# Gate2's modulation moved into quarters 1 and 2 of an MLP, and the last quarter's weight sums made by adding transfers

## The chip, the cores and the metric

The kernel runs on one core of a Trainium2 chip. The metric is the time of one execution on the device, in microseconds (us). Its engines are named here as in the profile: PE (TensorE, matrix products), DVE (VectorE), ACT (ScalarE), POOL (GpSimd), and SP (SyncE), whose queue issues the transfers. Sixteen DMA engines carry them out.

## The reference, cut to what matters

One layer of a decoder on 512 positions with 1024 features, in f32: a mixer (a recurrent branch and an attention branch, merged by gates), then an MLP with 4096 hidden features. The six vectors of the modulation come from one small product with a large weight matrix; `gate2` is the last of them and is used only in the last line.

```python
mod = (c_act @ w_ada[l] + b_ada[l])[:, None, :]
shift1, scale1, gate1, shift2, scale2, gate2 = jnp.split(mod, N_MOD, axis=-1)
...
x = x + gate1 * (merged @ w_out[l])

h2 = rms_norm(x) * (1.0 + scale2) + shift2
ff = jnp.square(jax.nn.relu(h2 @ w_ff1[l])) @ w_ff2[l]
x = x + gate2 * ff
```

## The kernel before, in words

Every f32 operand of a product is split into a high part (a cast to fp32r, on ACT) and a low part (the rest, on DVE); three matmuls, high x high, low x high and high x low, make one product (`mm3`, lines 127 to 131). A weight block of 128 x 1024 is loaded by SP into one of three slots (tag "w" of `wpool`), cast on ACT (`wh`, L122) and its rest taken on DVE (`wl`, L123), each with two buffers (`load_w`, lines 114 to 125).

The modulation is not computed on PE. `ada_chunk(j, k)` (lines 184 to 189) loads 128 x 1024 weights for 128 columns of vector j into a slot of the same tag "w" and multiplies and reduces them on DVE (L188) into one column of `mod`. j = 5 is gate2, of eight blocks; the column of block n is read at the very end, as `mcol(5, n)`.

The MLP goes in four quarters of 1024 hidden features (lines 1025 to 1040). In a quarter, `hidden` (858 to 868) computes eight hidden blocks f1_q_0 to f1_q_7 of 128 features by 512 positions; ACT applies relu and the square. Three blocks of the next quarter are computed ahead among the products, by `beside`, so that five remain in the hidden stage proper. Then `out_product` (870 to 1008) multiplies the quarter's hidden features by its share of `w_ff2`. This is a 2 x 2 block product with seven block products instead of eight (a Winograd scheme): p1 to p7 and sums of blocks. The four blocks of the hidden features are A[r][k] (256 positions by 512 features), the four of the weights b(k, c), each held in two tiles of 128 x 4 x 256 (512 KB each). The weights' sums are

- t1 = b(0,0) + b(0,1), for p5
- t2 = t1 + b(1,1), for p6
- t3 = b(0,1) + b(1,1), for p7
- t4 = t2 + b(1,0), for p4, which in the last quarter is `last_product`, called pl.

`sums` (945 to 948) makes them on DVE in place, two instructions (L948) each; b(0,0), b(1,0) and b(1,1) are used unsummed for p1, p2 and p3. The b tiles have eight slots (tag "b"), and a new quarter's tile takes a slot when the last reader of its old tile is done. `split_b` (893 to 907) splits each tile as above (L904 on ACT, L905 on DVE); the first tile of a product has two buffers of its own (p_0h, p_0l), the second shares those of `load_w` (p_1h, p_1l).

A product writes two PSUM banks X, Y or Z, and `add_c` (911 to 918) adds them on DVE to the f32 sums C[r][c][t] in SBUF. p5 goes to Z and p3 adds onto Z after C[1][1] has taken p5's result; X is used so by p1, p6, p7 and p4, Y by p2 (`second`). In quarter 3, p2 stands second, and at the end `finish` (1012 to 1023) transposes C on PE, multiplies by gate2 and adds to `x1` (L1020); `last_product` does the same with pl from PSUM (L941); both store to `out`.

The order on each engine is made by a scheduler, which takes the program's order and a priority: the casts, splits and sums stand inside `tc.high_priority(HP)` and are placed far ahead of their program order. Each engine then works its list strictly in order and waits at semaphores.

Of the kernel before, what the change touches and what calls it, by code (L numbers as in the profile page):

```python
# [16 lines left out]
F32 = mybir.dt.float32  # L17
# [4 lines left out]
ALU = mybir.AluOpType  # L22
AX = mybir.AxisListType

P = 128
S = 512
D = 1024
KC = D // P
# [25 lines left out]
def build(tc, out, x, xT_in, c, pos, vecs, reps, ada, w_xr, w_xr7, w_qk, w_v, w_gr, w_gm, w_lru,  # L54
          w_pr, w_pa, w_out, w_ff1, w_ff2):
    nc = tc.nc
    from contextlib import ExitStack

    with ExitStack() as es:
# [714 lines left out]
        acc = t_("acc", tag="a")  # L774
# [70 lines left out]
        ff = es.enter_context(tc.tile_pool(name="ff", bufs=1))  # L845
# [12 lines left out]
        def hidden(qd, ahead):  # L858

            raw = [ff.tile([P, 4, S], F32, name=f"r2_{qd}_{c}", tag="raw", bufs=2) for c in range(2)]  # L860
            for n in range(KC):
                rl = raw[n // 4][:, n % 4, :]
                if n < len(ahead):
                    nc.scalar.activation(rl, ahead[n], AF.Square)
                else:
                    hidden_relu(qd, n, rl)
                    nc.scalar.activation(rl, rl, AF.Square)
            return raw

        def out_product(qd, raw, beside):  # L870
            A = [[raw[k][:, :, r * H2:(r + 1) * H2] for k in range(2)] for r in range(2)]
            B = {}

            def get_b(k, c):
                if (k, c) not in B:
                    B[k, c] = []
                    for hf in range(2):
                        b = ff.tile([P, 4, 2 * P], F32, name=f"b{qd}_{k}{c}{hf}", tag="b", bufs=8)
                        k0 = (4 * k + 2 * hf) * P
                        nc.sync.dma_start(b, w_ff2[qd, 4 * c:4 * c + 4, :, k0:k0 + 2 * P].rearrange("n p f -> p n f"))  # L880
                        B[k, c].append(b)
                return B[k, c]

            def split_a(src, name, parts=1):
                ah = ff.tile([P, 4, H2], F32R, name=f"{name}h{qd}", tag="ah", bufs=3)
# [34 lines left out]
            def product(name, a, bs, ps, first):  # L920

                fs = [split_b(b, f"{name}_{qd}_{i}", i) for i, b in enumerate(bs)]
                for hf in range(2):
                    for t in range(2):
                        for kk in range(2):
                            k = 2 * hf + kk
                            ts = slice(t * P, (t + 1) * P)
                            mm3(ps[t], a[0][:, k, ts], a[1][:, k, ts], fs[hf][0][:, kk], fs[hf][1][:, kk],
                                first and k == 0, k == 3, not first)

            def last_product(a, bs):

                fs = [split_b(b, f"pl_{i}", i) for i, b in enumerate(bs)]
                for n in range(4):
                    ps = bank(f"pl{n}")[:, :H2]
                    fc = slice(n * P, (n + 1) * P)
                    for k in range(4):
                        wh, wl = (w[:, k % 2, fc] for w in fs[k // 2])
                        mm3(ps, wh, wl, a[0][:, k], a[1][:, k], k == 0, k == 3)
                    cols = slice(H2, S)  # L940
                    nc.vector.scalar_tensor_tensor(x1[n][:, cols], ps, mcol(5, n), x1[n][:, cols],  # L941
                                                   op0=ALU.mult, op1=ALU.add)
                    nc.sync.dma_start(out[n][:, cols], x1[n][:, cols])

            def sums(dsts, srcs):
                with tc.high_priority(HP):
                    for d, s_ in zip(dsts, srcs):
                        nc.vector.tensor_tensor(d, d, s_, op=ALU.add)  # L948
# [16 lines left out]

            if qd == 3:
                second()
            b12 = get_b(0, 1)
            sums(b11, b12)
            Z = [bank(f"Z{qd}_{t}") for t in range(2)]  # L970
            product("p5", s1, b11, Z, True)
            beside()
            with tc.high_priority(HP):
                nc.vector.tensor_tensor(sx, sx, A[0][0], op=ALU.subtract)
                s2 = split_a(sx, "s2")
            add_c(1, 1, Z, 1)
            b22 = get_b(1, 1)
            sums(b11, b22)
            product("p6", s2, b11, X, False)
            beside()  # L980
            with tc.high_priority(HP):
                nc.vector.tensor_tensor(sx, sx, A[0][1], op=ALU.add)
                s4 = split_a(sx, "s4")
            add_c(0, 1, X, -1)
            product("p3", s4, b22, Z, False)
            nc.vector.tensor_tensor(A[0][0], A[0][0], A[1][0], op=ALU.subtract)
            s3 = split_a(A[0][0], "s3")
            add_c(0, 1, Z, 1)
            sums(b12, b22)
            product("p7", s3, b12, X, False)  # L990
            add_c(1, 1, X, -1)
            if qd < 3:
                second()
            a22 = split_a(A[1][1], "a22")
            sums(b11, get_b(1, 0))
            if qd < 3:
                product("p4", a22, b11, X, False)
                add_c(1, 0, X, 1)
                return

# [4 lines left out]
                finish(n, 2, 4, False)  # L1005
            for n in range(4, KC):
                finish(n, 0, 4)
            last_product(a22, b11)

        n_fin = [0]  # L1010

# [13 lines left out]
        ahead = []  # L1025
        for qd in range(4):
            raw = hidden(qd, ahead)
            if qd == 0:
                for n in range(KC):
                    ada_chunk(5, n)  # L1030
            ahead = []

            def beside():

                if qd < 3:
                    ahead.append(t_(f"ahead{qd + 1}_{len(ahead)}"))
                    hidden_relu(qd + 1, len(ahead) - 1, ahead[-1])

            beside()
            out_product(qd, raw, beside)  # L1040
# [66 lines left out]
```

## Time and profile before

| | us |
|---|---|
| three timed runs | 893.14, 896.8, 897.4 (median 896.8) |
| the profiled execution, its own time | 894.77 |
| its span, first to last instruction | 893.0 |
| PE busy (share of the span) | 867.7 (97%) |
| DVE busy | 657.4 (74%) |
| ACT busy | 448.3 (50%) |
| POOL busy | 2.2 (0%) |

PE's granted clock is at its upper level nearly throughout (mean 0.998). The MLP begins near 555 us. Quarter 0's first product p1 starts at 595.8, quarter 3's at 843.2; quarters 1 and 2 are alike and 81.6 us apart.

How to read the rows below: a row of the timeline gives the start, the duration, the engine, the line, the operation with its tiles (output <- inputs, buffer numbers left out, so that p_0h stands for the first tile's high part of whatever product), and in brackets for how long the engine had been idle and what released it. Matmuls overlap, so that durations of single ones are longer than the spacing of their starts. A row with x2 holds two instructions in a row.

### The profile page before, as it was taken

The page shows a single profiled execution, that of the slowest core. Times are in us where ns is not written, and L with a number is a line of the kernel's source. Part 1 is how long each engine was busy: PE and PEld are TensorE (multiplying, and loading weights), DVE is VectorE, ACT ScalarE, POOL GpSimd, SP SyncE. Part 2 cuts the span into 40 slices and gives each one's busy share as a digit, 9 for nine tenths or more (in the row PEclk, how much of TensorE's full clock was granted, in tenths as well). Part 3 has the DMA queues.
Part 4 walks back from the last instruction along what each step waited for, and adds up shares of the span by engine and source line. Part 5 has one row for each costly group of instructions (what it writes and reads, how often), then busy time and mean ns, then how long its engine had stood idle before and what let it go on. Part 6 is the DMA issues. An engine that isn't in the chain of part 4 may idle for free.

```text
span 893.0 us, 11189 instructions
## 1 busy us (share of the span) xinstructions
PE 867.7 (97%) x4012; PEld 707.0 (79%) x4012; DVE 657.4 (74%) x1227; ACT 448.3 (50%) x748; POOL 2.2 (0%) x40
## 2 busy tenths in 40 slices
PE   6999999999999999999999999989999999999988
PEld 3888888687878878877778888878888888888867
DVE  6972983499969855895868566879646883876597
ACT  6663544895536533534543343746545544553541
POOL 0000000000000000000000000000000000000000
PEclk9999999999999999999999999999999999999999
DMA  8932236321255474448745332772421342233002
GB/s 318 353 142 97 92 116 144 120 70 48 95 127 158 137 213 146 142 136 206 246 155 183 135 119 78 273 237 95 163 99 48 118 142 95 72 117 118 1 1 94
DMA packets 54874, 121.56 MB, mean 136 GB/s; under 512 B 5666, under 2 KB 23202, under 8 KB 54820
## 3 DMA queue, kind: packets, MB, share of 16 engines
q1 hardware_dynamic: 54820, 120.87, 41.9%
q8 instruction: 31, 0.51, 0.2%
q14 instruction: 23, 0.19, 0.1%
HBM read 106.17 MB, written 2.10 MB: 121 GB/s over the span
## 4 chain that ended last, share of the span: by engine, by line
PE 74%; DVE 16%; DMA 5%; ACT 2%; issue 2%; SPq 0%; DVEq 0%; ACTq 0%
PE f L129 5%; PE f L130 5%; PE f L131 5%; DMA ada<-in_ada 3%; DVE wl L123 3%; PE X L131 3%; PE X L130 3%; PE X L129 3%; PE qk L131 2%; PE qk L129 2%; PE qk L130 2%; PE xr L129 2%; PE xr L131 2%; PE xr L130 2%; PE wo L130 2%
## 5 line engine op out<-in xcount | busy, mean ns | idle before, releaser
L122 ACT CAST wh<-w 128x1024 fp32r<-128x1024 f32 (+1 forms) x113 | 117.9, 1043 | 214.6 <-issue 56.2
L123 DVE TENSOR_TENSOR wl<-w,wh 128x1024 fp32r<-128x1024 f32 (+1 forms) x113 | 137.0, 1213 | 87.7 <-ACT wh L122 86.6
L129 PE MATMUL f<-h2h,wh 128*128 128x512 f32 x240 | 93.0, 390 | 2.3 <-ACT wh L122 2.3
L131 PE MATMUL f<-h2h,wl 128*128 128x512 f32 x240 | 93.5, 390 | 0.4 <-DVE wl L123 0.4
L130 PE MATMUL f<-h2l,wh 128*128 128x512 f32 x240 | 93.2, 389 | 0.0
L129 PEld LDWEIGHTS f<-h2h,wh 128*128 128x128 f32 x240 | 45.1, 188 | 12.0 <-ACT wh L122 2.7
L131 PEld LDWEIGHTS f<-h2h,wl 128*128 128x128 f32 x240 | 45.1, 188 | 10.0 <-DVE wl L123 0.8
L188 DVE CUSTOM_DVE_ANT_0 ada<-ada,cb,bada 128x1024 f32<-128x1024 f32 x32 | 41.0, 1281 | 16.1 <-DMA ada<-in_ada 16.1
L130 PEld LDWEIGHTS f<-h2l,wh 128*128 128x128 f32 x240 | 45.1, 188 | 9.3
L131 PE MATMUL gm<-hh,wl 128*128 128x512 f32 x128 | 51.3, 401 | 0.0
L129 PE MATMUL gm<-hh,wh 128*128 128x512 f32 x128 | 51.1, 399 | 0.0
L130 PE MATMUL gm<-hl,wh 128*128 128x512 f32 x128 | 50.9, 398 | 0.0
L129 PE MATMUL qk<-wh,hh 128*128 128x512 f32 x128 | 50.8, 398 | 0.0
L131 PE MATMUL qk<-wh,hl 128*128 128x512 f32 x128 | 50.6, 395 | 0.0
L130 PE MATMUL qk<-wl,hh 128*128 128x512 f32 x128 | 50.2, 393 | 0.0
L588 ACT ACTIVATE e<-e,nm 128x128 f32<-128x128 f32 (+3 forms) x64 | 35.8, 561 | 28.7 <-DVE nm L586 28.4
L905 DVE TENSOR_TENSOR p_1l<-b,p_1h 128x1024 fp32r<-128x1024 f32 x27 | 33.0, 1223 | 21.8 <-ACT p_1h L904 21.8
L904 ACT CAST p_0h<-b 128x1024 fp32r<-128x1024 f32 x27 | 28.5, 1054 | 27.2 <-PE X L131 14.0
L904 ACT CAST p_1h<-b 128x1024 fp32r<-128x1024 f32 x27 | 28.3, 1050 | 27.3 <-PE f L130 24.5
L905 DVE TENSOR_TENSOR p_0l<-b,p_0h 128x1024 fp32r<-128x1024 f32 x27 | 33.0, 1222 | 11.7 <-ACT p_0h L904 11.6
L948 DVE TENSOR_TENSOR b<-b,b 128x1024 f32<-128x1024 f32 x32 | 38.7, 1220 | 0.1
L586 DVE CUSTOM_DVE_ANT_0 e<-sc,mask 128x128 f32<-128x128 f32 (+3 forms) x64 | 30.3, 486 | 10.4 <-PE sc L581 10.4
(438 smaller groups left out, 2169.8 us busy)
## 6 DMA issues: line engine op xcount, KB each, us to landing
ada<-in_ada SPq DMA_DIRECT2D x32, 512.0 KB, 4.2
w<-in_w_ff SPq DMA_DIRECT2D x32, 512.0 KB, 3.2
b<-in_w_ff SPq DMA_DIRECT2D x32, 512.0 KB, 3.5
ada<-in_ada SPq DMA_DIRECT2D x32, 256.0 KB, 5.8
w<-in_w_qk SPq DMA_DIRECT2D x16, 512.0 KB, 3.3
w<-in_w_gm SPq DMA_DIRECT2D x16, 512.0 KB, 3.6
w<-in_w_gr SPq DMA_DIRECT2D x8, 512.0 KB, 3.2
w<-in_w_v SPq DMA_DIRECT2D x8, 512.0 KB, 3.2
```

The source lines that it names most:

```text
L122: i_w = nc.scalar.copy(wh[:, :n], w[:, :n])
L123: nc.vector.tensor_tensor(wl[:, :n], w[:, :n], f32(wh)[:, :n], op=ALU.subtract)
L129: nc.tensor.matmul(ps, lh, rh, start=first, stop=False, skip_group_check=more)
L130: nc.tensor.matmul(ps, lh, rl, start=False, stop=False, skip_group_check=more)
L131: nc.tensor.matmul(ps, ll, rh, start=False, stop=last, skip_group_check=more)
L188: nc.vector.tensor_tensor_reduce(w, w, cb, 1.0, bada[:, col:col + 1], op0=ALU.mult, op1=ALU.add, accum_out=mod[:, col:col + 1])
L586: nc.vector.tensor_tensor_reduce(e[:, :n], ps[m][:, :n], mask[:, S - n:], 1.0, 1e30, op0=ALU.add, op1=ALU.min, accum_out=nm)
L588: nc.scalar.activation(e[:, :n], e[:, :n], AF.Exp, bias=nm, scale=-1.0, accum_out=sums[:, m:m + 1])
L904: nc.scalar.copy(v4(wh), v)
L905: nc.vector.tensor_tensor(v4(wl), v, f32(v4(wh)), op=ALU.subtract)
L948: nc.vector.tensor_tensor(d, d, s_, op=ALU.add)
```

## The change

Two parts. The first takes gate2's eight `ada_chunk` calls from behind quarter 0's hidden stage and puts four each into `hidden` of quarters 1 and 2, one behind each of the hidden blocks 4 to 7. The second, in quarter 3 alone (`by_dma`), makes the sums t1, t2, t3 and t4 not on DVE: a fresh tile is loaded by SP with the first block, and further blocks are added into it by transfers that POOL issues with `accum_op=ALU.add`. t2 is loaded anew from b(0,0), and gets b(0,1) and b(1,1) one after the other; t4 adds b(1,0) into t2's tiles once p6 has split them. That makes twelve plain loads by SP instead of eight in this quarter, and ten adding transfers.

```diff
@@ -865,21 +865,48 @@
                 else:
                     hidden_relu(qd, n, rl)
                     nc.scalar.activation(rl, rl, AF.Square)
+                if qd in (1, 2) and n >= 4:
+                    ada_chunk(5, 4 * (qd - 1) + n - 4)
             return raw
 
         def out_product(qd, raw, beside):
             A = [[raw[k][:, :, r * H2:(r + 1) * H2] for k in range(2)] for r in range(2)]
             B = {}
 
+            def src_b(k, c, hf):
+                k0 = (4 * k + 2 * hf) * P
+                return w_ff2[qd, 4 * c:4 * c + 4, :, k0:k0 + 2 * P].rearrange("n p f -> p n f")
+
+            def load_b(name, *parts):
+
+                res = []
+                for hf in range(2):
+                    b = ff.tile([P, 4, 2 * P], F32, name=f"b{qd}_{name}{hf}", tag="b", bufs=8)
+                    nc.sync.dma_start(b, src_b(*parts[0], hf))
+                    for p_ in parts[1:]:
+                        nc.gpsimd.dma_start(b, src_b(*p_, hf), accum_op=ALU.add)
+                    res.append(b)
+                return res
+
             def get_b(k, c):
                 if (k, c) not in B:
-                    B[k, c] = []
-                    for hf in range(2):
-                        b = ff.tile([P, 4, 2 * P], F32, name=f"b{qd}_{k}{c}{hf}", tag="b", bufs=8)
-                        k0 = (4 * k + 2 * hf) * P
-                        nc.sync.dma_start(b, w_ff2[qd, 4 * c:4 * c + 4, :, k0:k0 + 2 * P].rearrange("n p f -> p n f"))
-                        B[k, c].append(b)
+                    B[k, c] = load_b(f"{k}{c}", (k, c))
                 return B[k, c]
+
+
+
+            by_dma = qd == 3
+
+            def b_sum(name, acc, k, c, *parts):
+
+                if not by_dma:
+                    sums(acc, get_b(k, c))
+                    return acc
+                if acc is None:
+                    return load_b(name, *parts, (k, c))
+                for hf, b in enumerate(acc):
+                    nc.gpsimd.dma_start(b, src_b(k, c, hf), accum_op=ALU.add)
+                return acc
 
             def split_a(src, name, parts=1):
                 ah = ff.tile([P, 4, H2], F32R, name=f"{name}h{qd}", tag="ah", bufs=3)
@@ -965,36 +992,34 @@
 
             if qd == 3:
                 second()
-            b12 = get_b(0, 1)
-            sums(b11, b12)
+            t1 = b_sum("t1", None if by_dma else b11, 0, 1, (0, 0))
             Z = [bank(f"Z{qd}_{t}") for t in range(2)]
-            product("p5", s1, b11, Z, True)
+            product("p5", s1, t1, Z, True)
             beside()
             with tc.high_priority(HP):
                 nc.vector.tensor_tensor(sx, sx, A[0][0], op=ALU.subtract)
                 s2 = split_a(sx, "s2")
             add_c(1, 1, Z, 1)
-            b22 = get_b(1, 1)
-            sums(b11, b22)
-            product("p6", s2, b11, X, False)
+            t2 = b_sum("t2", None if by_dma else t1, 1, 1, (0, 0), (0, 1))
+            product("p6", s2, t2, X, False)
             beside()
             with tc.high_priority(HP):
                 nc.vector.tensor_tensor(sx, sx, A[0][1], op=ALU.add)
                 s4 = split_a(sx, "s4")
             add_c(0, 1, X, -1)
-            product("p3", s4, b22, Z, False)
+            product("p3", s4, get_b(1, 1), Z, False)
             nc.vector.tensor_tensor(A[0][0], A[0][0], A[1][0], op=ALU.subtract)
             s3 = split_a(A[0][0], "s3")
             add_c(0, 1, Z, 1)
-            sums(b12, b22)
-            product("p7", s3, b12, X, False)
+            t3 = b_sum("t3", None if by_dma else get_b(0, 1), 1, 1, (0, 1))
+            product("p7", s3, t3, X, False)
             add_c(1, 1, X, -1)
             if qd < 3:
                 second()
             a22 = split_a(A[1][1], "a22")
-            sums(b11, get_b(1, 0))
+            t4 = b_sum("t4", t2, 1, 0)
             if qd < 3:
-                product("p4", a22, b11, X, False)
+                product("p4", a22, t4, X, False)
                 add_c(1, 0, X, 1)
                 return
 
@@ -1005,7 +1030,7 @@
                 finish(n, 2, 4, False)
             for n in range(4, KC):
                 finish(n, 0, 4)
-            last_product(a22, b11)
+            last_product(a22, t4)
 
         n_fin = [0]
 
@@ -1025,9 +1050,6 @@
         ahead = []
         for qd in range(4):
             raw = hidden(qd, ahead)
-            if qd == 0:
-                for n in range(KC):
-                    ada_chunk(5, n)
             ahead = []
 
             def beside():
```

SP's list in quarter 0 (w88 to w93 are f1 blocks, w89 that of f1_1_0; ada40 to ada47 are gate2's eight; b0 are weights of this quarter's products). Before:

```order
L118 DMA w88_5705<-in_w_ff1 128x1024
L187 DMA ada40_5738<-in_ada 128x1024
L880 DMA b0_101_6093<-in_w_ff2 128x4x256
L187 DMA ada41_5741<-in_ada 128x1024
...
L187 DMA ada47_5759<-in_ada 128x1024
L118 DMA w89_5763<-in_w_ff1 128x1024
L118 DMA w90_5891<-in_w_ff1 128x1024
```

Now, with the place in quarter 1 where three of the blocks went:

```order
L118 DMA w88_5705<-in_w_ff1 128x1024
L118 DMA w89_5739<-in_w_ff1 128x1024
L885 DMA b0_101_6069<-in_w_ff2 128x4x256
L118 DMA w90_5867<-in_w_ff1 128x1024
...
L885 DMA b1_101_6658<-in_w_ff2 128x4x256
L187 DMA ada41_6252<-in_ada 128x1024
L118 DMA w95_6255<-in_w_ff1 128x1024
L187 DMA ada42_6288<-in_ada 128x1024
L118 DMA w96_6291<-in_w_ff1 128x1024
L187 DMA ada43_6324<-in_ada 128x1024
L118 DMA w97_6328<-in_w_ff1 128x1024
```

w89 has moved ahead of all gate2 blocks; ada40 now stands behind the first block of quarter 1 (b1_000), and ada41 to ada43 alternate with f1 blocks. Quarter 2 has the same pattern with ada44 to ada47.

DVE's list in quarter 3, from the splits of p3 on (b3_000 and b3_001 hold t2, then t4; b3_010 and b3_011 hold t3). Before:

```order
L905 TENSOR_TENSOR p3_3_0l_7687<-b3_110_7641,p3_3_0h_7686 128x1024
L918 TENSOR_TENSOR C001_5525<-C001_5525,X3_1_7494 128x512
L905 TENSOR_TENSOR p3_3_1l_7691<-b3_111_7643,p3_3_1h_7690 128x1024
L948 TENSOR_TENSOR b3_000_7495<-b3_000_7495,b3_100_7556 128x1024
L948 TENSOR_TENSOR b3_001_7497<-b3_001_7497,b3_101_7558 128x1024
L905 TENSOR_TENSOR p7_3_0l_7728<-b3_010_7594,p7_3_0h_7727 128x1024
L918 TENSOR_TENSOR C000_5524<-C000_5524,Y3_0_7554 128x512
L905 TENSOR_TENSOR p7_3_1l_7732<-b3_011_7596,p7_3_1h_7731 128x1024
L918 TENSOR_TENSOR C001_5525<-C001_5525,Y3_1_7555 128x512
L918 TENSOR_TENSOR C110_5530<-C110_5530,Z3_0_7600 128x512
```

Now:

```order
L945 TENSOR_TENSOR C000_5524<-C000_5524,Y3_0_7554 128x512
L932 TENSOR_TENSOR p3_3_0l_7693<-b3_110_7688,p3_3_0h_7692 128x1024
L945 TENSOR_TENSOR C001_5525<-C001_5525,Y3_1_7555 128x512
L945 TENSOR_TENSOR C110_5530<-C110_5530,Z3_0_7600 128x512
L932 TENSOR_TENSOR p3_3_1l_7697<-b3_111_7690,p3_3_1h_7696 128x1024
L945 TENSOR_TENSOR C111_5531<-C111_5531,Z3_1_7601 128x512
L1011 TENSOR_TENSOR r2_3_0_7323<-r2_3_0_7323 128x4x256
L932 TENSOR_TENSOR p7_3_0l_7738<-b3_t30_7731,p7_3_0h_7737 128x1024
```

The sums are gone, and the additions of Y and Z into C have moved ahead of p7's splits. On PE the four transposes of C[0][0] have moved from behind p6 to behind p7, the product next to the last.

POOL's list, which before ended with the last of the memsets that write the rotary frequencies, long before the MLP; now it goes on with the ten adds, first tile and second tile of t1, t2 (twice), t3 and t4:

```order
L362 MEMSET fr_640 128x4 x32
L887 DMA b3_t10_7594<-in_w_ff2 128x4x256
L887 DMA b3_t11_7597<-in_w_ff2 128x4x256
L887 DMA b3_t20_7641<-in_w_ff2 128x4x256
L887 DMA b3_t21_7645<-in_w_ff2 128x4x256
...
L887 DMA b3_t30_7731<-in_w_ff2 128x4x256
L887 DMA b3_t31_7734<-in_w_ff2 128x4x256
L908 DMA b3_t20_7641<-in_w_ff2 128x4x256
L908 DMA b3_t21_7645<-in_w_ff2 128x4x256
```

The second add of each t2 tile waits for the first; t3's tiles take the slots that p1's and p2's second tiles leave.

## Rows read from the trace of the kernel before

**Rows 1.** Waits of PE, 555 us to the end: us in total, times, longest.

```profile
PE cT L1017 <- DVE C L918: 2.6, 2, 1.3
PE f L129 <- ACT wh L122: 2.3, 1, 2.3
PE f L131 <- DVE wl L123: 0.4, 1, 0.4
PE Z L129 <- DVE C L918: 0.3, 1, 0.3
```

**Rows 2.** Stretches: us, busy time of each engine, clock, DMA share, GB/s.

```profile
655.00:682.00 27.00, 27.00 (x120) 22.37 (x120) 8.20 (x9) 11.96 (x17) 0.00 (x0) 1.00 0.29 98
...
843.00:866.00 23.00, 22.27 (x98) 17.92 (x96) 21.68 (x22) 13.31 (x15) 0.00 (x0) 1.00 0.00 0
866.00:869.00 3.00, 0.92 (x5) 0.48 (x5) 3.00 (x5) 0.36 (x1) 0.00 (x0) 1.00 0.00 0
```

**Rows 3.** Timeline, quarter 0: start us, us, engine line op, idle before and releaser.

```profile
595.73 6.77 SPq L118 DMA_DIRECT2D w<-in_w_ff  x4
...
600.94 0.50 PE L129 MATMUL f<-h2h,wh 128*128 128x512 f32 x1 [2.29 <-ACT wh L122]
```

**Rows 4.** Timeline, DVE in quarter 3.

```profile
862.35 2.35 DVE L948 TENSOR_TENSOR b<-b,b 128x1024 f32<-128x1024 f32 x2
...
865.76 0.68 DVE L918 TENSOR_TENSOR C<-C,Y 128x512 f32<-128x512 f32 x1
...
867.53 0.68 DVE L918 TENSOR_TENSOR C<-C,Y 128x512 f32<-128x512 f32 x1
```

**Rows 5.** The page's groups, the reduction of a modulation block: busy us, mean ns.

```profile
L188 DVE CUSTOM_DVE_ANT_0 ada<-ada,cb,bada 128x1024 f32<-128x1024 f32 x32 | 41.0, 1281 | 16.1 <-DMA ada<-in_ada 16.1
```

**Rows 6.** Timeline, hidden stage of quarter 1: casts and split of f1 blocks.

```profile
658.21 1.05 ACT L122 CAST wh<-w 128x1024 fp32r<-128x1024 f32 x1 [3.62 <-PE f L130]
...
659.29 1.23 DVE L123 TENSOR_TENSOR wl<-w,wh 128x1024 fp32r<-128x1024 f32 x1 [3.94 <-ACT wh L122]
...
663.65 1.05 ACT L122 CAST wh<-w 128x1024 fp32r<-128x1024 f32 x1 [2.58 <-PE f L130]
```

**Rows 7.** The page's DMA issues: KB each, median us from issue to landing.

```profile
ada<-in_ada SPq DMA_DIRECT2D x32, 512.0 KB, 4.2
...
b<-in_w_ff SPq DMA_DIRECT2D x32, 512.0 KB, 3.5
...
w<-in_w_xr SPq DMA_DIRECT2D x8, 448.0 KB, 6.3
...
out_dram<-x SPq DMA_DIRECT2D x8, 128.0 KB, 1.7
```

**Rows 8.** Timeline, DVE in the tail.

```profile
879.06 2.65 DVE L918 TENSOR_TENSOR C<-C,X 128x512 f32<-128x512 f32 x4
881.63 0.87 DVE L1020 SCALAR_TENSOR_TENSOR x<-cT,mod,x 128x256 f32<-128x256 f32 x2
...
885.39 2.93 DVE L1020 SCALAR_TENSOR_TENSOR x<-cT,mod,x 128x512 f32<-128x512 f32 x4
...
889.35 0.48 DVE L941 SCALAR_TENSOR_TENSOR x<-pl,mod,x 128x256 f32<-128x256 f32 x1 [0.64 <-PE pl L131]
```

**Rows 9.** Timeline, b blocks of quarter 3: loads, splits and casts.

```profile
799.49 0.37 SPq L880 DMA_DIRECT2D b<-in_w_ff  x1
...
807.95 0.37 SPq L880 DMA_DIRECT2D b<-in_w_ff  x1
...
844.25 1.23 DVE L905 TENSOR_TENSOR p_1l<-b,p_1h 128x1024 fp32r<-128x1024 f32 x1 [1.70 <-ACT p_1h L904]
...
857.21 1.22 DVE L905 TENSOR_TENSOR p_1l<-b,p_1h 128x1024 fp32r<-128x1024 f32 x1
...
865.31 1.04 ACT L904 CAST p_1h<-b 128x1024 fp32r<-128x1024 f32 x1 [1.21 <-PE X L131]
...
874.87 1.04 ACT L904 CAST pl_1h<-b 128x1024 fp32r<-128x1024 f32 x1
```

## The prediction

> **What bounds the kernel now.** I read the waits of TensorE (PE) over the MLP first, then the busy times in stretches around them, and last the timeline at the two places where PE waits; elsewhere in the MLP PE's work is dense and only its amount counts, which the change leaves as it is. From 555 us to the end PE waits for four causes [rows 1]: 2.3 + 0.4 us for a weight block's split in quarter 0, and 2.6 + 0.3 us for additions into C by VectorE (DVE) in quarter 3. A hidden stage (655 to 682) has no wait, PE is busy 27.00 of 27 us and DVE 8.20; at 866 to 869 it is the other way round, DVE 3.00 of 3.00 and PE 0.92, and before it DVE has worked 21.68 of 23 us [rows 2]. The granted clock is 1.00 (the 2.4 GHz level) in all of them.
>
> Quarter 0: SyncE (SP) issues the eight gate2 blocks first, each when one of the three shared slots is free, and only at 595.73 the block of f1_1_0, which PE computes ahead for quarter 1; its first matmul starts at 600.94, after 2.29 us of idle, behind the split by ScalarE (ACT) [rows 3]. Quarter 3: the additions of Y into C[0][0], at 865.76 and 867.53, stand behind two sums of b (862.35) and the splits of p7 on DVE [rows 4], and the transposes that read C[0][0] wait for them.
>
> **Gate2's blocks.** Eight 512 KB transfers and eight multiply-and-reduce instructions leave quarter 0; four go to quarter 1's and four to quarter 2's list. By the order, f1_1_0's block (w89) now stands directly behind w88 and ahead of all gate2 blocks, so it lands some 15 us before PE asks for it. What goes is 2.3 + 0.4 = **2.7 us**. What is late next there is DVE, but it then does what it does in quarters 1 and 2, where no PE wait stands.
>
> What the blocks cost where they go: DVE time is 8 x 1.28 us [rows 5], as before. Six of the eight lie in hidden stages, where DVE idles 18.8 of 27 us [rows 2]. ada40 and ada44 stand among the products, behind the first split of p7; bounds 0 and their own 2 x 1.28 = 2.6 us. I take 0: what stands behind them on DVE is for p2 and the second halves of p3 and p7, most of a product (24 matmuls, 5.4 us) away. The transfers are moved into SP's queue between the f1 blocks and share their three slots. A block is cast every 5.44 us (663.65 - 658.21), and the split that frees a slot for w96 ends at 659.29 + 1.23 = 660.5 [rows 6]. Landing takes 3.5 us, a gate2 block 4.2 [rows 7]: 664.0, against a cast due at 663.65 + 5.44 = 669.1; 5.1 us are spare. ada43 waits in SP's queue until ada42 is reduced, near 662, and lands at 666.3; w97 behind it is issued near 666, lands by 669.5 and is due at 674.5. DVE takes its instructions in order and would stand at ada43 for 0.4 us, with nothing due before 670. Cost 0; if that cover goes, stalls of quarter 0's size, 2.3 us each.
>
> **The sums by transfer.** In quarter 3 eight sums leave DVE: two in the idle hidden stage, two near 840, and four (two take 2.35 us [rows 4]) between 852 and 865, where DVE is without a gap. Those four bring everything behind them forward by up to 4.5 us. In the order C000 + Y0 now stands before the first split of p3 and C001 + Y1 right behind it, and the transposes that waited stand behind p7, so p3 starts as p6 ends. Its bank Z is drained in time: p5 ends one whole product before p6 does, and C110 and C111 are then two additions. What goes is 2.6 + 0.3 = **2.9 us**. What is late next is the tail. Its first addition after p7, at 879.06, comes at 876.2; from there DVE has four additions (881.63 - 879.06 = 2.57), eight finishes of half 0.87, four of a quarter of 2.93, four of the last product at 0.48: 10.9 us, done at 887.1. PE's last matmul releases the last addition at 889.35 - 2.9 = 886.5, done at 886.9 [rows 8]. So DVE sets the end, 887.1 against 889.8: of the 2.9 us, **2.7 us** hold.
>
> What they cost: four more plain loads on SP and ten adding transfers on the queue of GpSimd (POOL), which had none. No row shows such an add. Below, it may land like the fastest row, 1.7 us; above, like the slowest one read twice, 2 x 6.3 = 12.6 [rows 7]. The nearest row is the same block's plain load, 3.5 us for 512 KB; against 1.7 for 128 KB that is 1.8 us for 384 KB more, and an add, which reads its destination as well, moves 512 KB more: 3.5 + 2.4 = **5.9 us**, my estimate. The Trainium skill ("DMA: Bandwidth & Descriptors", section "Anatomy of one DMA — SWDGE (gpsimd) path") gives 2.0 us plus the bytes at 436 GB/s for a transfer issued by GpSimd, an estimate of 3.2 us for 512 KB; no run here shows it, and by it every spare time below would be longer and the sum the same.
>
> Due times [rows 9]: t2's second half is loaded at 807.95, landed at 811.5, twice added by 823.3; its split starts at 857.21. Half 1 of t3 takes the slot of p2's second block, split until 844.25 + 1.23 = 845.5: loaded 849.0, added 854.9, its cast due at 865.31 - 2.9 = 862.4. t4 may be added into t2's second half only when p6 has split it, 857.21 + 1.22 = 858.4: added 864.3, its cast due at 874.87 - 2.9 = 872.0. The least spare is 7.5 us. All ten stand in one queue; even one after another from 803.0 (the first load, 799.49 + 3.5) they end at 803.0 + 59 = 862. PE stays covered; cost 0.
>
> **Sum.** 893.0 - 2.7 - 2.7 = 887.6 us of span. The profiled execution took 894.77 us, 1.8 above its span; the three timed runs have their median at 896.8, 2.0 above that. I set out from the middle of the two, 895.8: 895.8 - 5.4 = **890.4 us**.
>
> **Rivals.**
> (b) The last quarter gives nothing: PE's wait only moves, from the additions to the tail or to a split of p3 or p7. For it: DVE still makes all splits of six products there, and the tail is already DVE's. Against: the four sums are 4.5 us, more than the 2.9 us of wait. 895.8 - 2.7 = 893.1.
> (c) Gate2 starves the f1 blocks: in quarters 1 and 2 every second slot holds a gate2 block. It decides once an f1 block lands more than 5.1 us late. For it: that is the mechanism of quarter 0's wait. Against: there eight stood in a row, here one between two blocks that are 5.44 us apart. With one 2.3 us stall in each of the two quarters: 890.4 + 4.6 = 895.0.
> (d) The slower side: the ten adds run strictly one at a time and each takes over (872.0 - 803.0) / 10 = 6.9 us. At 8.4 us, twice gate2's 4.2, the tenth ends at 887.0, 12.1 us after the cast of 874.87 that reads it, and the last product is late by that: 895.8 - 2.7 + 12.1 = 905.2. For it: one queue, a kind of transfer not seen here. Against: the plain blocks land in 3.5 us, and adds into different tiles wait for nothing of each other.
> (e) The adds do not proceed while DVE works. From 844.25 to 869 DVE has no gap [rows 2]; t3's half 1 would start only when DVE itself runs dry at p7's second split, near 864, and land at 869.9 where 862.4 was due: 890.4 + 7.5 = 897.9. Against: adds have 40 us before that in which DVE idles often. The Trainium skill ("SBUF — State Buffer", section "SBUF: two separate sides") warns that GpSimd cannot write the descriptors of its transfers while DVE runs in a mode that takes both ports. DVE's rows here are two-input ones, 1.23 us for 1024 elements [rows 9] where 512 take 0.68 [rows 4], so no doubled mode shows, and by that rule the adds would not be held.
>
> **Chances.** Forecast 0.56, (b) 0.13, (c) 0.09, (d) 0.16, (e) 0.06. About 0.5%, 4.5 us, is what a measurement can tell from no change, so faster means under 891.3. The forecast lies 0.9 us beyond that, and the runs shown spread over 4 us: of its 0.56 I give 0.44 to faster and 0.12 to same; (b) and (c) go to same but for 0.02 to faster, (e) 0.04 to same and 0.02 to slower, (d) to slower: faster 0.46, same 0.36, slower 0.18. The forecast's own range is 888 to 893. That of 8 in 10 reaches down to 887 and up into (d), to 902, since adds of 6.9 to 8.1 us lie below that.
>
> **What would show it.** Right: no PE wait for a weight split near 600; the additions of Y done before p6 ends; PE unbroken from quarter 3's p1 to the transposes; adds that land in 4 to 8 us, each before its cast would start. Wrong: ACT waiting for an add (d, e), PE waiting for a split of an f1 block in quarters 1 or 2 (c), or waits in the tail as long as those that went (b).

## The result, and the profile after

| | before | changed |
|---|---|---|
| runs, us | 893.14, 894.68, 896.8, 897.4 | 886.77, 888.32, 888.33, 888.9 |
| median | 895.74 | 888.33 |
| ratio, 95% interval | | 0.9917 [0.9888, 0.9946] |
| profiled execution, its span | 894.77, 893.0 | 886.77, 885.0 |
| PE busy, DVE busy, POOL busy | 867.7, 657.4, 2.2 | 865.4, 648.3, 15.1 |

The forecast was 890.4, in a range of 887 to 902. The changed kernel is 7.4 us faster, where the sum gave 5.4.

The waits of PE from 555 us to the end, which were four causes [rows 1], are now one:

```profile
PE f L131 <- DVE wl L123: 0.4, 1, 0.4
```

The stretches that answer to [rows 2]: the hidden stage of quarter 1, which now also reduces gate2's blocks on DVE, and the last quarter up to p3 and just behind its start (us; busy time of PE, PEld, DVE, ACT, POOL; clock; DMA share; GB/s).

```profile
650.00:677.00 27.00, 27.00 (x121) 22.36 (x120) 11.91 (x15) 11.57 (x17) 0.00 (x0) 1.00 0.47 156
838.50:861.50 23.00, 23.00 (x103) 19.06 (x102) 21.62 (x24) 14.71 (x17) 5.08 (x4) 1.00 0.66 115
861.50:864.50 3.00, 3.00 (x15) 2.49 (x14) 3.00 (x4) 2.02 (x3) 0.00 (x0) 1.00 0.00 0
```

In the hidden stage DVE works 11.91 us instead of 8.20 [rows 2], close to three gate2 blocks more at 1.28 us each, and PE still has no gap. In the last quarter DVE has 21.6 of 23 us, as before; but PE no longer stands behind it.

Fixed points of the program, from which distances can be read: the short wait in quarter 0's hidden stage, the first matmul of quarter 3's p1, and the last instruction of DVE (889.35 before, [rows 8]). Timeline of the kernel before, then of the changed one, with the additions of Y that answer to [rows 4], p3's first matmul, and the tail's first addition that answers to 879.06 in [rows 8]:

```profile
574.32 0.50 PE L131 MATMUL f<-h2h,wl 128*128 128x512 f32 x1 [0.37 <-DVE wl L123]
...
843.19 0.39 PE L129 MATMUL X<-p_0h,a11h 128*128 128x512 f32 x1
...
868.96 0.47 PE L129 MATMUL Z<-p_0h,s4h 128*128 128x512 f32 x1 [0.25 <-DVE C L918]
```

```profile
572.48 0.50 PE L131 MATMUL f<-h2h,wl 128*128 128x512 f32 x1 [0.37 <-DVE wl L123]
...
838.72 0.39 PE L129 MATMUL X<-p_0h,a11h 128*128 128x512 f32 x1
...
853.33 0.68 DVE L945 TENSOR_TENSOR C<-C,Y 128x512 f32<-128x512 f32 x1
...
855.06 0.68 DVE L945 TENSOR_TENSOR C<-C,Y 128x512 f32<-128x512 f32 x1
...
860.48 0.39 PE L129 MATMUL Z<-p_0h,s4h 128*128 128x512 f32 x1
...
870.20 2.65 DVE L945 TENSOR_TENSOR C<-C,X 128x512 f32<-128x512 f32 x4 [1.66 <-PE X L131]
...
881.03 0.48 DVE L968 SCALAR_TENSOR_TENSOR x<-pl,mod,x 128x256 f32<-128x256 f32 x1 [0.28 <-PE pl L131]
```

Call A the distance from the first point to the second, B that from the second to the end of DVE's last instruction. A falls from 843.19 - 574.32 = 268.87 to 266.24, by 2.63: gate2's part. B falls from 46.64 to 42.79, by 3.85: the sums' part. The first point itself comes 1.84 us sooner, though the instructions ahead of it stand in the same order in both kernels.

The adding transfers, from the DMA issues (KB, median us to landing), POOL's timeline with ACT's cast that reads the last of them, and the plain loads that SP issued at the same time as the first ones:

```profile
b<-in_w_ff SPq DMA_DIRECT2D x30, 512.0 KB, 3.5
...
b_t<-in_w_ff POOLq DMA_DIRECT2D x10, 512.0 KB, 6.3
```

```profile
799.29 1.42 POOL L887 DMA_DIRECT2D b_t<-in_w_ff  x1 [796.36 <-DVE p_1l L932]
803.33 1.28 POOL L887 DMA_DIRECT2D b_t<-in_w_ff  x1 [2.63 <-DMA b_t<-in_w_ff]
808.48 1.27 POOL L887 DMA_DIRECT2D b_t<-in_w_ff  x1 [3.86 <-issue]
809.98 1.28 POOL L887 DMA_DIRECT2D b_t<-in_w_ff  x1 [0.23 <-issue]
819.07 1.27 POOL L887 DMA_DIRECT2D b_t<-in_w_ff  x1 [7.82 <-DMA b_t<-in_w_ff]
823.58 1.28 POOL L887 DMA_DIRECT2D b_t<-in_w_ff  x1 [3.24 <-DMA b_t<-in_w_ff]
...
850.84 1.26 POOL L908 DMA_DIRECT2D b_t<-in_w_ff  x1 [1.87 <-DVE p_0l L932]
853.71 1.28 POOL L908 DMA_DIRECT2D b_t<-in_w_ff  x1 [1.61 <-DVE p_1l L932]
...
866.16 1.06 ACT L931 CAST pl_1h<-b_t 128x1024 fp32r<-128x1024 f32 x1 [1.66 <-PE Z L131]
```

```profile
795.02 8.82 SPq L885 DMA_DIRECT2D b_t<-in_w_ff  x4
805.90 0.37 SPq L885 DMA_DIRECT2D b<-in_w_ff  x1
808.62 0.34 SPq L118 DMA_DIRECT2D w<-in_w_ff  x1
811.34 0.37 SPq L885 DMA_DIRECT2D b<-in_w_ff  x1
814.06 0.34 SPq L118 DMA_DIRECT2D w<-in_w_ff  x1
```

The add issued at 853.71 landed in 5.6 us, at 859.3; its cast at 866.16 waits for PE, not for it. The first four adds, issued beside these loads, landed in 8.5, 9.7, 10.3 and 13.3 us, outside the 4 to 8 us that the prediction gave as a sign of being right; the other six took 5.6 to 6.9 us. ACT waits for none of the ten.

### The profile page after: what moved, and what is told of

The parts are those of the page before. It is cut to its first block, busy times and chain, and to the rows that moved or that the text cites. A ratio compares the mean times of both kernels' runs of the same rounds, so it can differ in the third digit from the quotient of the medians.

```text
span 885.0 us, 11232 instructions
## 1 busy us (share of the span) xinstructions
PE 865.4 (98%) x4012; PEld 707.4 (80%) x4012; DVE 648.3 (73%) x1219; ACT 448.7 (51%) x748; POOL 15.1 (2%) x50
## 4 chain that ended last, share of the span: by engine, by line
PE 79%; DVE 14%; DMA 3%; ACT 2%; issue 1%; SPq 0%; ACTq 0%; DVEq 0%
PE f L131 6%; PE f L129 6%; PE f L130 6%; PE X L131 3%; PE X L130 3%; PE X L129 3%; DVE wl L123 3%; PE qk L131 2%; PE qk L129 2%; PE qk L130 2%; PE xr L129 2%; PE gm L129 2%; PE xr L131 2%; PE xr L130 2%; PE wo L130 2%; PE wo L129 2%
## 5 line engine op out<-in xcount | busy, mean ns | idle before, releaser
L932 DVE TENSOR_TENSOR p_1l<-b,p_1h 128x1024 fp32r<-128x1024 f32 x24 | 29.4, 1223 | 26.2 <-ACT p_1h L931 26.1
L931 ACT CAST p_1h<-b 128x1024 fp32r<-128x1024 f32 x24 | 25.2, 1051 | 31.0 <-PE f L130 29.3
L932 DVE TENSOR_TENSOR p_0l<-b,p_0h 128x1024 fp32r<-128x1024 f32 x24 | 29.3, 1222 | 15.0 <-ACT p_0h L931 15.0
L931 ACT CAST p_0h<-b 128x1024 fp32r<-128x1024 f32 x24 | 25.3, 1055 | 24.2 <-PE X L131 12.4
L975 DVE TENSOR_TENSOR b<-b,b 128x1024 f32<-128x1024 f32 x24 | 29.1, 1219 | 0.1
```

The costliest lines, as they stand in the source:

```text
L931: nc.scalar.copy(v4(wh), v)
L932: nc.vector.tensor_tensor(v4(wl), v, f32(v4(wh)), op=ALU.subtract)
```

## The experiments

Each ran against the kernel before on the same chip. A and B are read from each kernel's profile as above; the clock is the mean granted clock over its timed runs (before: 0.995 over 49 runs).

| | median us | ratio, 95% interval | A | B | clock |
|---|---|---|---|---|---|
| before | 897.3 to 898.1 | | 268.87 | 46.64 | 0.995 |
| changed, again | 888.81 | 0.9916 [0.9902, 0.9931] | 266.25 | 42.81 | 0.998 |
| gate2 only | 894.87 | 0.9967 [0.9951, 0.9983] | 266.23 | 49.09 | 0.995 |
| sums only | 889.8 | 0.9927 [0.9902, 0.9953] | 271.13 | 42.77 | 0.998 |
| no adds | 889.49 | 0.9910 [0.9889, 0.9931] | 266.25 | 42.78 | 0.997 |
| t3, t4 only | 890.41 | 0.9927 [0.9905, 0.9950] | 266.26 | 43.42 | 0.997 |
| gate2, filled | 892.99 | 0.9957 [0.9939, 0.9974] | 266.28 | 46.64 | 0.997 |
| early finish | 889.78 | 0.9926 [0.9911, 0.9941] | 266.24 | 42.90 | 0.997 |
| t4 thrice | 895.19 | 0.9984 [0.9968, 0.9999] | 266.24 | 49.22 | 0.994 |
| t4 twice | 887.86 | 0.9892 [0.9878, 0.9906] | 266.27 | 42.78 | 0.999 |
| mixer filled | 889.03 | 0.9909 [0.9895, 0.9924] | 266.26 | 42.78 | 0.999 |
| all quarters | 892.39 | 0.9938 [0.9916, 0.9961] | 267.64 | 42.79 | 0.998 |
| gate2 in one quarter | 890.49 | 0.9916 [0.9903, 0.9930] | 266.24 | 42.79 | 0.997 |

**Gate2 alone.**

```diff
-            by_dma = qd == 3
+            by_dma = False
```

> Changed kernel with the sums of the last quarter back on DVE, so that only gate2's blocks have moved. Theory (two independent parts, and what is left of the measured 7.4 us is the mixer's own scatter): quarter 0 is 2.6 us shorter (PE's wait of 2.3 us and the broken order of matmuls behind it), quarter 3 as before with its waits of 2.6 and 0.3 us: 895.7 - 2.6 = 893.1, ratio 0.997. Rival 1 (the 1.8 us by which the mixer was shorter in the changed kernel's trace belong to the change): 891.3, and the MLP's first f1 matmul near 560.5 instead of 562.3. Rival 2 (gate2 does nothing, quarter 0's time goes to the next wait): 895.7.

A is 266.23: the theory holds, to 0.02 us of the changed kernel. Rivals 1 and 2 fall: the first point lies at 575.89, later than before. But B is 49.09, 2.45 more than in the kernel before, with the same two waits. The stretch behind them in this trace:

```profile
864.00:867.00 3.00, 0.64 (x3) 0.20 (x2) 3.00 (x4) 1.04 (x1) 0.00 (x0) 0.90 0.00 0
867.00:873.00 6.00, 5.81 (x14) 4.38 (x15) 4.45 (x8) 0.00 (x0) 0.00 (x0) 0.50 0.14 46
```

PE did 0.64 us of work in 3, and then the granted clock stands at 0.50, the 1.2 GHz level; 14 matmuls fit where 27 do at 1.00. No theory had this.

**The sums alone.**

```diff
-                if qd in (1, 2) and n >= 4:
-                    ada_chunk(5, 4 * (qd - 1) + n - 4)
...
+            if qd == 0:
+                for n in range(KC):
+                    ada_chunk(5, n)
```

> Changed kernel with gate2's eight blocks back behind quarter 0's hidden stage, so that only the sums of the last quarter are made by transfers. Theory (independent parts): quarter 0's wait of 2.3 us for w89's cast is back, quarter 3's waits are gone and the end comes 3.85 us sooner from its first product on: 895.7 - 3.9 = 891.8, ratio 0.9957. Forecast's own size of this term, 2.7: 893.0. Rival 1 (mixer's 1.8 us belong to the change): 890.0. Rival 2 (the two parts need each other): no gain, 895.7.

B is 42.77, so the two parts do not need each other. Quarter 0's wait is back, 2.98 us here, and again the clock falls behind it:

```profile
601.00:604.50 3.50, 0.53 (x3) 0.10 (x1) 1.89 (x4) 1.09 (x2) 0.00 (x0) 1.00 0.80 266
605.00:608.00 3.00, 3.00 (x9) 2.33 (x8) 3.00 (x4) 1.87 (x3) 0.00 (x0) 0.50 0.66 217
```

The kernel before has waits of nearly this size at both places, and in its profiled execution no fall behind them: a fall follows such a wait in some executions only. Its stretches behind the wait of quarter 0, and behind that of quarter 3:

```profile
601.00:605.00 4.00, 4.00 (x18) 3.27 (x19) 4.00 (x5) 2.31 (x3) 0.00 (x0) 1.00 0.69 242
...
869.00:872.00 3.00, 3.00 (x14) 2.48 (x15) 3.00 (x5) 0.00 (x0) 0.00 (x0) 1.00 0.02 5
```

By time, 0.9927, it is faster than the 0.9957 of the theory, and not told apart from both parts together (0.9916). That gate2's blocks add to the sums is shown by A alone.

**No adds.**

```diff
-                    for p_ in parts[1:]:
-                        nc.gpsimd.dma_start(b, src_b(*p_, hf), accum_op=ALU.add)
...
-                for hf, b in enumerate(acc):
-                    nc.gpsimd.dma_start(b, src_b(k, c, hf), accum_op=ALU.add)
```

> Changed kernel with the ten adding transfers left out: the last quarter's four sums are not made at all, its plain loads stay. Theory (adds are wholly covered, least spare some 7 us): the same time as the changed kernel, 888.3, ratio 0.9917, within 0.5 us, and DVE's and PE's rows in the last quarter the same. Rival (the adds cost something after all, by their traffic or by holding DVE or the casts): 1 to 3 us faster than the changed kernel, 885 to 887.

B is 42.78 without the ten adds and 42.79 with them. They cost nothing; the rival falls.

**t3 and t4 only.**

```diff
-                if not by_dma:
+                if not by_dma or name in ("t1", "t2"):
...
-            t1 = b_sum("t1", None if by_dma else b11, 0, 1, (0, 0))
+            t1 = b_sum("t1", b11, 0, 1, (0, 0))
...
-            t2 = b_sum("t2", None if by_dma else t1, 1, 1, (0, 0), (0, 1))
+            t2 = b_sum("t2", t1, 1, 1, (0, 0), (0, 1))
```

> Changed kernel with t1 and t2 of the last quarter back on DVE; only t3 and t4 by transfers (four adds instead of ten). Theory: between 852 and 865 of the kernel before, where DVE had no gap, t2's and t4's sums stood, 2.35 us each; t4's alone are gone here, and PE's waits for the additions of Y (2.6 us) with them since 2.35 us cover most of it, but DVE enters the tail later than in the changed kernel: 889.0 to 890.0. Rival 1 (each sum that leaves the gapless stretch is worth its own time): half of 3.85 is given back, 890.2. Rival 2 (t4's sums alone decide): 888.3 as the changed kernel.

B is 43.42: 3.22 of the 3.85 us come from these. Rival 1 falls, and the theory's "later into the tail" is 0.6 us. The additions of Y start 19.16 us behind p1's start here, against 22.57 before and 14.61 in the changed kernel; that is still ahead of p6's end, and p3 starts at 21.92 without a wait. What counts is where these additions stand, not how much leaves DVE.

**Gate2 with the wait filled** (the sums on DVE as in gate2 alone; matmuls in quarter 3 behind p6, whose results are not read).

```diff
-            by_dma = qd == 3
+            by_dma = False
...
+                pd = bank("fill", "o", 1)
+                with tc.high_priority(HP):
+                    for i in range(10):
+                        m = nc.tensor.matmul(pd, h2[i % 8][0][:, :P], h2[i % 8][0], start=True, stop=True)
...
```

> Gate2's move alone, as in the first experiment, with ten matmuls that nobody reads put between p6 and the transposes of the last quarter, where PE stood still for 2.6 us. Theory (PE's stillness there is followed by a stretch at the lower clock level in many executions, 867 to 873 us in the first experiment's trace, and this costs more than the wait): the additions come as late as before and p3 starts where it did, but behind it the granted clock stays 1.00: 2 us less than gate2's move alone, ratio 0.9945, mean clock 0.997. Rival 1 (the clock falls at random, whatever PE did): 0.9967 again, mean clock 0.995. Rival 2 (the fillers only push p3 back): 0.998.

```profile
862.00:866.00 4.00, 3.40 (x17) 2.31 (x15) 4.00 (x6) 1.06 (x1) 0.00 (x0) 1.00 0.00 0
866.00:872.00 6.00, 6.00 (x27) 4.94 (x28) 5.40 (x8) 2.97 (x4) 0.00 (x0) 1.00 0.13 44
```

B is 46.64, that of the kernel before to the hundredth: the additions still set p3's start, the fillers cost nothing, and the 2.45 us of the fall are gone in this execution. One trace does not show that the fillers did it, since that of the kernel before has no fall either; the mean clock, 0.997 over eight runs against 0.995 over twelve, speaks for it. By time alone, 0.9957 against 0.9967, the two are not told apart.

**t4 thrice.**

```diff
-                for hf, b in enumerate(acc):
-                    nc.gpsimd.dma_start(b, src_b(k, c, hf), accum_op=ALU.add)
+                for rep in range(3):
+                    for hf, b in enumerate(acc):
+                        nc.gpsimd.dma_start(b, src_b(k, c, hf), accum_op=ALU.add)
```

> Changed kernel in which the add that makes t4 is done three times over for each tile (t4 gets b(1,0) three times). Theory (spare time 6.8 us, adds of 5.6 us one behind the other in the one queue): the last lands near 871.6, 5.4 us after ACT would have cast it at 866.2; ACT waits for an add, DVE's split stands ahead of the additions of the tail, which begin 3.7 us later: 892 where the changed kernel has 888.3, some 0.4% more. Rival 1 (adds of the two tiles run side by side): last landing near 866, no loss. Rival 2 (DVE holds adds off while it works): 6 us and more.

POOL's and ACT's timeline, the adds into the two tiles by turns, three into each, and the cast that reads the first tile:

```profile
853.59 1.26 POOL L909 DMA_DIRECT2D b_t<-in_w_ff  x1 [2.06 <-DVE p_0l L933]
856.46 1.28 POOL L909 DMA_DIRECT2D b_t<-in_w_ff  x1 [1.60 <-DVE p_1l L933]
859.79 1.26 POOL L909 DMA_DIRECT2D b_t<-in_w_ff  x1 [2.06 <-DMA b_t<-in_w_ff]
862.70 1.28 POOL L909 DMA_DIRECT2D b_t<-in_w_ff  x1 [1.65 <-DMA b_t<-in_w_ff]
866.28 1.26 POOL L909 DMA_DIRECT2D b_t<-in_w_ff  x1 [2.31 <-DMA b_t<-in_w_ff]
868.95 1.28 POOL L909 DMA_DIRECT2D b_t<-in_w_ff  x1 [1.40 <-DMA b_t<-in_w_ff]
```

```profile
872.35 1.05 ACT L932 CAST pl_0h<-b_t 128x1024 fp32r<-128x1024 f32 x1 [7.14 <-DMA b_t<-in_w_ff]
```

ACT waits for an add, as named: 6.2 and 6.5 us pass from one add into a tile to the next, and the tail's additions come 35.79 us behind p1's start instead of 31.48, 4.3 later (3.7 expected). But it is the chain of three into one tile that takes the time, not one queue for all: the adds of the two tiles, 2.7 to 3.6 us apart, are under way together and each lands in 5.9 to 6.2 us, as rival 1 had it, though not without loss. B grows by 6.4; the rest of it falls where PE stands in the tail and then runs at 0.50:

```profile
875.00:880.00 5.00, 1.81 (x11) 1.20 (x10) 4.73 (x8) 1.04 (x1) 0.00 (x0) 0.88 0.00 0
880.00:883.00 3.00, 2.82 (x13) 2.82 (x14) 1.87 (x5) 0.00 (x0) 0.00 (x0) 0.50 0.40 131
```

**t4 twice.**

```diff
-                for hf, b in enumerate(acc):
-                    nc.gpsimd.dma_start(b, src_b(k, c, hf), accum_op=ALU.add)
+                for rep in range(2):
+                    for hf, b in enumerate(acc):
+                        nc.gpsimd.dma_start(b, src_b(k, c, hf), accum_op=ALU.add)
```

> Changed kernel in which the add that makes t4 is done twice for each tile (t4 gets b(1,0) twice). Theory (6.8 us of spare time, one more add takes 6.3 us from issue to the next): the last lands near 865.6, just ahead of its cast at 866.2; time as the changed kernel, 0.9916 to 0.9925, and the one with three adds, 0.9984, lies behind the edge. Rival (adds near the tail cost something each, through DVE or the memory): half of what three cost, 0.995.

B is 42.78, nothing lost: the spare time lies between one add more and two. The ratio, 0.9892, is no gain of this kernel, which does more work than the changed one; its A and B are the same. So much can two sets of runs differ.

**Early finish** (the same loop is gone from behind p7).

```diff
+            if qd == 3:
+                for n in range(4):
+                    finish(n, 0, 2)
             t3 = b_sum("t3", None if by_dma else get_b(0, 1), 1, 1, (0, 1))
```

> Changed kernel with the four finishes of C[0][0] put behind p3 instead of behind p7. Theory (DVE sets the end, and idles 1.66 us ahead of its first addition after p7): the four finishes, 1.7 us, go into that idle time, the tail is 0.5 to 1.5 us shorter since PE's last product then sets it: 0.9905. Rival (PE's order in p7 is broken three times by the transposes, which costs what is won): as the changed kernel, 0.9915.

B is 42.90: a miss. DVE's four finishes went into its idle time, but the transposes broke p7's order on PE; the tail's first addition came 32.42 us behind p1's start instead of 31.48, and the shorter tail only gave that back.

**Mixer filled** (`filler` issues so many matmuls of `h` whose results are not read).

```diff
+            last = filler(bank("fillA", "o", 1), 8, pins["pg"]) if n == 3 else None
...
+            last = filler(pins["po"][:, P:3 * P], 12, pins["yT"]) if (hd, i) == (6, 1) else None
```

> Changed kernel with matmuls that nobody reads put into two waits of PE in the mixer, 2.1 us near 158 and 1.6 us near 422, behind which several traces show 3.4 us at the lower clock level. Theory (stillness of PE brings the fall): no stretch at 0.50 near 160 and 423, mean clock 0.999 or more, a fall saved is 1.7 us, so 1.5 to 3 us less than the changed kernel: ratio 0.989. Rival 1 (falls come at random): 0.9916, mean clock 0.998. Rival 2 (the fillers delay what stands behind): 0.993.

The stretches behind the two places, with the fillers, and below without them, in the early-finish kernel's trace:

```profile
160.00:164.00 4.00, 4.00 (x16) 2.68 (x16) 1.20 (x3) 2.99 (x6) 0.00 (x0) 1.00 0.82 316
423.00:426.00 3.00, 2.89 (x19) 2.28 (x17) 3.00 (x8) 2.24 (x6) 0.00 (x0) 1.00 0.82 279
```

```profile
160.00:164.00 4.00, 4.00 (x12) 2.75 (x11) 1.20 (x3) 3.18 (x6) 0.00 (x0) 0.62 0.81 316
423.00:426.00 3.00, 2.50 (x13) 2.30 (x12) 2.60 (x7) 3.00 (x7) 0.00 (x0) 0.63 0.30 87
```

There is no fall in the one trace; but the trace of all quarters, below, has none at either place without a filler (clock 1.00), and the time is that of the changed kernel: 0.9909 against 0.9916. As a faster version it is not shown.

**All quarters.**

```diff
-            by_dma = qd == 3
+            by_dma = True
```

> Changed kernel with the sums made by transfers in all four quarters: forty adds instead of ten, 24 more sums (29 us) off DVE. Theory (in quarters 0 to 2 PE waits for nothing of DVE's, so nothing is to be won; adds there have as much spare time as in the last quarter): as the changed kernel, 0.991 to 0.992. Rival (quarter 0 begins without an earlier quarter's time to load ahead, twelve plain loads and ten adds there come late, and split casts wait for them): a wait of some 5 us in quarter 0, 0.997.

A grows by 1.4: ACT waits 3.9 us for an add in quarter 0, and PE's waits for splits of f1 blocks are 1.1 us in three instead of 0.4 in one (matmuls start 0.59 and 0.96 us behind the one ahead at the two new ones, where 0.23 is usual, and the next 0.34: 1.3 of the 1.4). Nothing is won; the runs, 0.9938, are rather slower, by more than A says. How much stays open.

**Gate2 in one quarter.**

```diff
-                if qd in (1, 2) and n >= 4:
-                    ada_chunk(5, 4 * (qd - 1) + n - 4)
+                if qd == 1 and n >= 4:
+                    ada_chunk(5, 2 * n - 8)
+                    ada_chunk(5, 2 * n - 7)
```

> Changed kernel with all of gate2's eight blocks in quarter 1, two behind each of the hidden blocks 4 to 7, none in quarter 2. Theory (three slots, an f1 block due every 5.44 us with 5.1 us to spare; a second gate2 block ahead of it takes about 4 us of that): no wait of PE or one under 1 us, 0.9916 to 0.993. Rival (two gate2 blocks between f1 blocks starve them as eight did in quarter 0): 2.3 us at three or four blocks, 7 to 9 us, near 1.0.

A is 266.24. ACT waits 1.03 us for one f1 block, PE for none. Rival (c) of the forecast would not have come about even at twice the load.

**The changed kernel again.**

> The changed kernel again, for the same runs of the kernel before as the next three. Theory (parts add; gate2 0.9967 by the first experiment, the sums 0.9927 by the second): 0.9894; mean granted clock near 0.997 where the kernel before showed 0.995. Rival (they overlap, the first measurement of 0.9917 is the truth): 0.992.

0.9916: the rival's number, by time. By A and B the parts are independent, and their sum is 6.48 us of 893, a ratio of 0.9927 at equal clock.

## Why the prediction was right, and where its sizes were off

**Gate2, 2.7 forecast, 2.63 measured.** The size is right partly by luck. The 0.4 us of [rows 1] that I counted here is the wait at 574.32, in quarter 0's first hidden blocks, and has nothing to do with w89; it is still there. In its place the wait of w89 was itself worth more than the 2.29 us that its row gives as idle. Matmuls start 0.23 us apart before it, but 2.68 and 0.34 at it, 2.56 more than two usual steps:

```profile
598.26 0.39 PE L131 MATMUL X<-p_0h,a11l 128*128 128x512 f32 x1
600.94 0.50 PE L129 MATMUL f<-h2h,wh 128*128 128x512 f32 x1 [2.29 <-ACT wh L122]
601.28 0.40 PE L130 MATMUL f<-h2l,wh 128*128 128x512 f32 x1
```

The blocks cost nothing where they went, as worked out.

**The sums, 2.7 forecast, 3.85 measured.** The mechanism was right; the step that failed is "Its first addition after p7, at 879.06, comes at 876.2". From p1's start it came 35.87 - 31.48 = 4.39 us sooner, not 2.9. I took off the waits alone. Between p6's end and p3 stood the four transposes too, and they left with the waits: p3 starts 25.77 - 21.76 = 4.01 us sooner. p3 and p7 together take 0.38 less: in the kernel before, the second matmul of p3 started 0.31 us behind the first, and in p7 two steps were 0.35 and 0.34, the first of them just as DVE had made s3's low part; 0.23 is usual, and all that the changed kernel has there. Of this the tail takes back 0.54 (11.31 us for the 10.77 before), since the transposes and finishes now lie there. That DVE goes on to set the end is not quite so: it idles 1.66 us for PE ahead of the first addition, and in the tail neither engine leads by much, as the early finish showed.

**The adds.** Cost 0, as forecast, with 6.8 us of spare time for t4 (7.7 forecast). The last four adds landed in 5.6 us each; 5.9 was estimated. The estimate of 3.2 us for these bytes by the Trainium skill ("DMA: Bandwidth & Descriptors", "Anatomy of one DMA — SWDGE (gpsimd) path") is too short for adds; the measurement decides. Rival (d), adds strictly one at a time, falls: those at 850.84 and 853.71 went into different tiles, were under way together and landed in 5.6 us each, and t4 thrice has six such. Slow adds there were, the four of 8.5 to 13.3 us; the plain loads issued among them, at 805.90 and 808.62, also took 7.7 and 6.7 us, where plain loads of these blocks have a median of 3.5 and 3.3. How much of that the adds did to each other and how much the loads, no run separates. t2's second half was added at about 829, not 823.3, and that mattered to nobody. The three adds show the price that (d) put on lateness. (e) falls: the add at 853.71 landed in 5.6 us, in a stretch with DVE busy 21.62 of 23. The trace agrees with the rule of the Trainium skill cited there ("SBUF — State Buffer", "SBUF: two separate sides"), as far as it goes: DVE's two-input rows held no add up.

**What no step had.** The sum was made from one execution in which the clock stood at 1.00 everywhere in the MLP. Three traces have a wait of PE of 1 us or more open in quarter 3: before (no fall), gate2 alone and t4 thrice (a fall behind it, the first worth 2.45 us). Of the eleven other traces, none falls between p1 of quarter 3 and the tail. The mean clock of the three kernels with such a wait is 0.994 to 0.995, that of the other ten 0.997 to 0.999. That a wait brings the fall is so supported, and by the filled one, but not proven: the wait in quarter 0 of the sums alone, with a fall in its trace, left that kernel's mean at 0.998.

How often a fall comes can be counted in the mixer, where all thirteen traces with the same mixer have the same two waits of PE. Behind that of 2.1 us near 158 the clock fell to 0.50 in eight of them, behind that of 1.6 and 0.5 us near 422 in nine. With neither fall the first point lies at 572.8 us (one trace), with one of them at 574.5 on average (seven), with both at 576.0 (five).

The clock also accounts for most of what is left over (7.4 to 8.5 us measured, 6.48 in A and B). The lower level is half the upper, so 893 us times the rise of the mean clock is an estimate of what fewer falls give back: 2.7 us for the changed kernel again, which with the 6.45 us of its A and B makes 9.1, where 8.5 was measured. Of the nine experiments without a fall in A or B, this sum is within 0.7 us of the measured difference in seven; it is 1.1 too high for the filled mixer and 2.1 for all quarters. Where a fall stands in A or B it is counted twice, and the sum is 2.9 to 3.5 us too low. My base of 895.8 was low in the same way: three later sets of the kernel before had medians of 897.3 to 898.1. What stays open is the rest of the mixer's scatter: with one fall, the first point still lies anywhere from 572.5 to 576.0 us.

## What to carry to other kernels

When an instruction's wait is removed, take off all that stood in the gap, not the wait alone, and add it where it goes: here that is 4.39 - 0.54 instead of 2.9. Measure a small edit by distances between two fixed points inside the traces (here they repeat to 0.05 us, where medians of the same program differ by 2). Work may be moved from a full engine onto a queue that idles if its due time is several transfers away; what counts is which instruction it stood ahead of, not how much of it there was.

## What the runs showed of the hardware that was not expected

A stand of PE of 2.6 us, in two halves with two transposes between them, was followed by the lower clock level in some executions and not in others, and one of 2.1 us in eight of thirteen. With ten matmuls of no use in the first gap the one trace there is stays at 1.00, and the mean clock is 0.997 instead of 0.995. And an adding transfer of 512 KB occupied POOL for 1.27 us at its issue and took 5.6 us where a plain load's median is 3.5. Two into different tiles, issued 2.9 us apart, still took 5.6 us each; four issued in a row among plain loads took 8.5 to 13.3 us.
